# Moving down-products, row products, the ranking of experts and an overflow loop in a mixture-of-experts kernel

## The chip, the core and the metric

The kernel runs on one core of one Trainium2 chip. Its engines are TensorE (PE; its weight loads are shown apart as PEld), VectorE (DVE), ScalarE (ACT), GpSimd (POOL) and SyncE (SP), which issues most DMAs. The metric is device time in microseconds (us), the median of several executions. Rows of a trace come from one profiled execution, counted from the start of its span.

## The reference

The reference is one layer of a decoder, for 512 rows of 1024 channels. Its first part mixes tokens (a gated recurrence and a sparse attention, merged and projected), and the change does not touch it. The second part is a mixture of experts:

```python
N_GROUPS = 4
EXP_PER_GROUP = 8          # 32 experts; one group per row, two experts in it
TOPK_IN_GROUP = 2
D_EXPERT = D_MODEL // 2    # 512
...
# per routed row:  h = silu(row @ exp_w1[e]) * (row @ exp_w3[e]);  y = h @ exp_w2[e]
# a row's two results are weighted and added; then residual and LayerNorm
```

The two commented lines put the expert's formula in short. With 512 rows and two experts each there are 1024 routed rows over 32 experts, unevenly. All of it is float32.

## The kernel before, in words

**Units.** The expert part works through 13 units, called first to thirteenth here (`n` = 0 to 12 in the code). A unit is 128 slots, shared by one, two or four experts. First `rank` sorts the experts by the number of their rows, so that the busiest get a whole unit, the middle ones half of one and the others a quarter. The first two units hold experts 0 to 3 and do not depend on the ranking; all later units load the experts that the ranking names. Rows beyond an expert's slots go to the overflow loop (below).

**A unit's work.** `gather` makes the products pgx, which pick the unit's rows out of x by one-hot matrices (pm) and leave them transposed in xe; it serves two coming units at a time. `up` (L1461) makes two sets of products p, rows by exp_w1 and by exp_w3; ACT takes the silu of the first set and DVE multiplies it by the second (s, L1469). `down_lhs` (L1472) transposes s (pat) and the weighted one-hot matrix pw (ptw) on PE; ACT copies the former (aT, L1477). `down` (L1496) makes the down-products py, weighs them (y) and splits them in two parts (yh, yl). `combine` (L1508) multiplies these by the 0/1 matrix pT and adds the result to the four row blocks of acc: the *row products* pcb, 16 per unit. A unit's row products are made one unit later. In the program the order on PE is, for each unit: up-products, row products of the unit before, gather (after every second unit), transposes, down-products.

**Weights.** An expert has 12 tiles of 128x1024 float32 (512 KB): four each of exp_w1, exp_w3 and exp_w2. They stand in a ring Q of 36 buffers, of which 12 hold other things at that time. SP issues their loads (L1270; of the last unit's exp_w2 L1267, cut by quarters of the columns) in program order, and each waits until the products that read the buffer's tile before are done. SP has eight DMA counters, named DMAHW0 to DMAHW7 in the listings below, and a load waits for the one that had its counter before.

**The sort.** `sort_experts` (L1371) stands behind the first unit's up-products. Four products on PE count the rows of each expert (pcnt), then DVE works out ranks, slots (`look`, which makes the one-hot's `lk`) and the overflow list. For the units to come `rel_to` (L1329) and `one_hots` prepare the matrices on DVE.

**The end.** In `quarter_up` (L1603) and `quarter_add` (L1613) the last unit's down-products are made in four quarters of 256 columns; behind each stand 16 row products, which add both the last unit's rows and those of the twelfth unit (`todo`) to acc. `squares` (L1600) on ACT prepares the norms, and the closing work from L1625 on scales and stores the rows. Between the third and the fourth quarter's row products stands `overflow` (L1521): a loop (L1526) that runs nblk times, once per block of 128 rows beyond their experts' slots, and loads each block's weights for itself. In the runs shown nblk is zero: no instruction of the loop's body is in the trace, only its branches. Two broadcasts of norm vectors (`row_bc`) are loaded by POOL ahead of the last unit's transposes.

All instructions stand in the order in which the code writes them; no scheduler moves them.

Of the kernel before, what the change touches and what calls it, by code (L numbers as in the profile page):

```python
# [21 lines left out]
F32 = mybir.dt.float32  # L22
# [5 lines left out]
OP = mybir.AluOpType  # L28
# [3 lines left out]
NT = T // 128  # L32
# [109 lines left out]
def hybrid_kernel(ctx, tc, a, out, dbg=None, stop=None):  # L142
# [17 lines left out]
    def S(name, dt=F32):  # L160
        return big.tile([128, 512], dt, name=name, tag="S", bufs=24)
# [1206 lines left out]
    ovf = cp.tile([128, 64], F32, name="ovf")  # L1368
    ovi = cp.tile([128, 64], I32, name="ovi")

    def sort_experts():  # L1371

        pcnt = PS("pcnt")
        for j in range(NT):
            mm(pcnt[:, 0:32], onesb, mb[:, j, :], j == 0, j == NT - 1)
        srt = S("srt")
        key, rk, base, cap_, t6, cnt = (srt[:, 32 * j:32 * j + 32] for j in range(6))
        V.tensor_copy(cnt, pcnt[:, 0:32])
        V.scalar_tensor_tensor(key, cnt, 32.0, iota[:, 0:32], op0=OP.mult, op1=OP.subtract)
        V.tensor_scalar(key[:, 0:4], iota[:, 0:4], -1.0, -100.0, op0=OP.mult, op1=OP.add)  # L1380
        big2 = S("cmpm").bitcast(BF).rearrange("p (e f) -> p e f", e=32)
        V.tensor_tensor(big2, key[:, None, :].to_broadcast([128, 32, 32]),
                        key.rearrange("p (e o) -> p e o", o=1).to_broadcast([128, 32, 32]), op=OP.is_gt)
        V.tensor_reduce(rk.rearrange("p (e o) -> p e o", o=1), big2, axis=AX.X, op=OP.add)

        V.tensor_tensor(big2, rk[:, None, :].to_broadcast([128, 32, 32]),
                        iota[:, 0:32].rearrange("p (e o) -> p e o", o=1).to_broadcast([128, 32, 32]), op=OP.is_equal)
        V.tensor_tensor(big2, big2, iota[:, None, 0:32].to_broadcast([128, 32, 32]), op=OP.mult)
        V.tensor_reduce(ovf[:, 0:32].rearrange("p (j o) -> p j o", o=1), big2, axis=AX.X, op=OP.add)
        V.tensor_copy(ovi[:, 0:32], ovf[:, 0:32])  # L1390
        t1 = S("t1")[:, :256].rearrange("p (c i e) -> p c i e", c=2, i=NT)

        def look(dst, table):

            V.tensor_tensor(t1, oh2, table[:, None, None, :].to_broadcast([128, 2, NT, 32]), op=OP.mult)
            V.tensor_reduce(dst.rearrange("p c (i o) -> p c i o", o=1), t1, axis=AX.X, op=OP.add)

        V.tensor_scalar(cap_, rk, 2.0, 64.0, op0=OP.is_lt, op1=OP.mult)
        V.tensor_scalar(t6, rk, 12.0, 32.0, op0=OP.is_lt, op1=OP.mult)
        V.tensor_add(cap_, cap_, t6)
        V.tensor_scalar(t6, rk, 28.0, 32.0, op0=OP.is_ge, op1=OP.mult)
        V.scalar_tensor_tensor(cap_, cap_, 32.0, t6, op0=OP.add, op1=OP.add)
        V.tensor_scalar(base, rk, 64.0, 128.0, op0=OP.mult, op1=OP.add)
        V.scalar_tensor_tensor(base, rk, 128.0, base, op0=OP.mult, op1=OP.min)
        V.tensor_scalar(t6, rk, 32.0, 512.0, op0=OP.mult, op1=OP.add)
        V.tensor_tensor(base, base, t6, op=OP.min)
        look(bst, base)  # L1410
        look(capt, cap_)
        V.tensor_tensor(far, pos, capt, op=OP.is_ge)
        V.tensor_add(slots, bst, pos)
        V.scalar_tensor_tensor(slots, far, 1e5, slots, op0=OP.mult, op1=OP.add)
        probe("slots", slots)


        ov = S("ov")
        need, incl, st0, t5 = ov[:, 0:32], ov[:, 32:64], ov[:, 64:96], ov[:, 96:128]
        V.tensor_sub(t5, cnt, cap_)  # L1420
        V.tensor_scalar(need, t5, 0.0, None, op0=OP.is_gt)
        for j in range(1, 4):
            V.scalar_tensor_tensor(need, t5, 128.0 * j, need, op0=OP.is_gt, op1=OP.add)
        V.tensor_tensor_scan(incl, need, need, 0.0, OP.add, OP.max)
        V.tensor_sub(st0, incl, need)
        look(ob, st0)
        V.scalar_tensor_tensor(oslots, ob, 128.0, pos, op0=OP.mult, op1=OP.add)
        V.tensor_sub(oslots, oslots, capt)
        V.tensor_scalar(far, far, 1e5, -1e5, op0=OP.mult, op1=OP.add)
        V.tensor_add(oslots, oslots, far)  # L1430
        le = S("le").bitcast(BF)[:, 0:NOV * 32].rearrange("p (j e) -> p j e", j=NOV)
        V.tensor_tensor(le, incl[:, None, :].to_broadcast([128, NOV, 32]),
                        iota[:, 0:NOV].rearrange("p (j o) -> p j o", o=1).to_broadcast([128, NOV, 32]), op=OP.is_le)
        V.tensor_copy(ovf[:, 32:33], incl[:, 31:32])
        V.tensor_reduce(ovf[:, 33:33 + NOV].rearrange("p (j o) -> p j o", o=1), le, axis=AX.X, op=OP.add)
        V.tensor_copy(ovi[:, 32:33 + NOV], ovf[:, 32:33 + NOV])
# [21 lines left out]
        t = w[k // 2]  # L1458
        return t[k % 2] if isinstance(t, list) else t[:, (k % 2) * 512:(k % 2 + 1) * 512]

    def up(xe, n0, ws, rhs=k1):  # L1461
        lhs = lambda k: xe[k // 2][:, k % 2, :]
        p1 = PS("p1")
        unit_mm(p1, lhs, n0, ws["exp_w1"], rhs, 8)
        s1 = S("s1")
        A.activation(s1, p1, AF.Silu)
        p3 = PS("p3")
        unit_mm(p3, lhs, n0, ws["exp_w3"], rhs, 8)
        V.tensor_mul(s1, s1, p3)  # L1469
        return s1  # L1470
# [22 lines left out]
        V.tensor_sub(yl, y, yh.bitcast(F32))  # L1493
        return yh, yl

    def down(act, ws, pw, rhs=k1):  # L1496
        aT, pT, cs_ = down_lhs(act, pw)
        pys = [PS("py") for _ in range(2)]
        m = 128 // len(ws["exp_w2"])
        for k in range(4):  # L1500
            for half in range(2):
                for x, w in enumerate(ws["exp_w2"]):
                    mm(pys[half][m * x:m * x + m, :], aT[:, k, m * x:m * x + m], rhs(w, 2 * k + half), k == 0, k == 3,
                       pos=(0, m * x) if m < 128 else None)
        ys = [weighted_halves(pys[half], cs_, half * 512, 512) for half in range(2)]
        return pT, ys
# [14 lines left out]
    def overflow():  # L1521
        ocnt = cp.tile([128, 1], F32, name="ocnt")
        V.memset(ocnt, 0.0)
        nonlocal S
        S, s_ring = (lambda name, dt=F32: Q(name, dt)[:, 0:512]), S
        with tc.For_i(0, nblk, 1) as jb:  # L1526
            ex = nc.sync.value_load(ovi[0:1, ds(jb + 33, 1)], min_val=0, max_val=NE - 1)
            rel = rel_to(oslots, ocnt)
# [12 lines left out]
                return get  # L1541
            act = up(xe, 0, {n: [stream(n)] for n in ("exp_w1", "exp_w3")}, lambda w, k: w(k))
            combine(*down(act, {"exp_w2": [stream("exp_w2")]}, pw, lambda w, h: w(h)))

            for i in range(NT):
                V.tensor_reduce(sums[:, i, 0:3], acc[i][:, 0:768].rearrange("p (q n) -> p q n", q=3), axis=AX.X, op=OP.add)
                squares(i, 0)
        S = s_ring


    units = [-2, -1] + ORDER
    todo, hots, nblk = None, None, None
    ws = w_first
    for n, u in enumerate(units):
        pw = weighted(rels.pop(u))
        nxt = units[n + 1:n + 3] if n % 2 == 1 else []
        if nxt:
            for x in nxt:
                rels[x] = rel_to(slots, 128.0 * x)
            hots = one_hots([rels[x] for x in nxt])  # L1560
        if n == 4:

            nblk = nc.values_load_multi_w_load_instructions(
                ovi[0:1, 32:33], min_val=0, max_val=NOV - 1,
                skip_runtime_bounds_check_because="a sum of fewer blocks than NOV")[1][0]
        act = up(xe, (n % 2) * 128, ws)
        if n == 0:
            sort_experts()
        w_now = ws
        if n + 1 < len(units):  # L1570
            v_ = units[n + 1]
            if v_ < 0:
                es = (2, 3)
            elif v_ < 2:
                es = (ev(v_),)
            elif v_ < 7:
                es = (ev(2 * v_ - 2), ev(2 * v_ - 1))
            else:
                es = tuple(ev(4 * v_ - 16 + x) for x in range(4))
            ws = load_unit(es, quarters=n + 2 == len(units))  # L1580
        if todo is not None and n + 1 < len(units):
            combine(*todo)
        if nxt:
            xe = gather(hots)
        if n + 1 < len(units):
            todo = down(act, w_now, pw)
    l2g = row_bc("l2g", a["ln2_g"])
    l2b = row_bc("l2b", a["ln2_b"])

# [22 lines left out]

    def quarter_add(q, y, i):  # L1613

        o = q % 2 * 256
        terms = [(todo[0], t[:, o:o + 256]) for t in todo[1][q // 2]] + [(pT, t) for t in y]
        pc_ = PS("pcb")[:, 0:256]
        for j, (p_, t) in enumerate(terms):
            mm(pc_, p_[:, i * 128:(i + 1) * 128], t, j == 0, j == 3)
        z = acc[i][:, q * 256:(q + 1) * 256]  # L1620
        V.tensor_tensor_reduce(out=z, in0=z, in1=pc_, scale=1.0, scalar=0.0, op0=OP.add, op1=OP.add,  # L1621
                               accum_out=sums[:, i, q:q + 1])
# [35 lines left out]
            V.tensor_scalar(nsh, sums[:, :, 0], -1.0 / 256, None, op0=OP.mult)  # L1658
    squares(2, 0)
    squares(3, 0)  # L1660
    overflow()
    A.preload_act_table_set("natural_log_exp_and_others")
    V.tensor_reduce(l3[:, :, 4:5], sums[:, :, 0:3], axis=AX.X, op=OP.add)
    for i in range(NT):
# [42 lines left out]
```

## Time and profile before

| | |
|---|---|
| median of 3 runs | 1275.64 us (1275.42 to 1276.81) |
| profiled execution | 1276.27 us, span 1274.4 us |
| PE busy | 1176.6 us (92%) |
| DVE busy | 697.5 us (55%) |
| ACT busy | 425.5 us (33%) |
| POOL busy | 123.4 us (10%) |
| DMA | 297 MB, mean 233 GB/s |

The shares are means over the whole span. The expert part is the last 500 us or so, and the page's slices, each a fortieth of the span (31.9 us), show how engines and DMA stand in it. Each product of two float32 operands has two rows in the trace (x32 for 16 products in the order); durations hold for the pairs as they stand.

### The profile page before, as it was taken

The numbers are of one execution on the slowest core, as the hardware profiler recorded it, in microseconds if no ns is written. First come the engines' busy times: TensorE is split into PE (matmuls) and PEld (weight loads), VectorE is DVE, ScalarE is ACT, GpSimd is POOL, SyncE is SP. The second block draws the span as 40 slices with busy tenths as digits, with TensorE's granted clock in tenths as the row PEclk, the third lists the DMA queues.
The fourth block names the chain that finished last, engine by engine and source line by source line (L and its number), as shares of the span: only waits on it lengthen the run. The fifth ranks groups of instructions, "written<-read, shape, count | busy, mean of one in ns | idle before, by whom it ended". The sixth has DMA issues, their size and how long they took to land. (4 is left out here: it accounts for less than half of the span.)

```text
span 1274.4 us, 18563 instructions
## 1 busy us (share of the span) xinstructions
PE 1176.6 (92%) x6663; PEld 813.2 (64%) x6663; DVE 697.5 (55%) x1621; ACT 425.5 (33%) x897; POOL 123.4 (10%) x179
## 2 busy tenths in 40 slices
PE   5999999999999999999979969999999899899993
PEld 4788898778888888878758953525335235143442
DVE  5564988887565665314596786534143143313436
ACT  5233666664536254554131421201102012010113
POOL 3011111111110011010250140000000000000002
PEclk9999999999999999999999979999999999999997
DMA  9954413324334153345425279799999999999991
GB/s 324 295 152 139 120 52 117 104 87 129 112 109 142 45 174 100 92 147 156 132 66 182 79 301 361 297 411 408 409 409 409 409 409 408 409 409 407 403 346 68
DMA packets 140863, 297.15 MB, mean 233 GB/s; under 512 B 11099, under 2 KB 82979, under 8 KB 140768
## 3 DMA queue, kind: packets, MB, share of 16 engines
q1 hardware_dynamic: 131296, 268.57, 57.5%
q0 software_dynamic: 8704, 25.00, 6.2%
q10 hardware_dynamic: 768, 2.37, 0.5%
q8 instruction: 53, 0.87, 0.3%
q14 instruction: 42, 0.34, 0.1%
HBM read 293.76 MB, written 4.76 MB: 234 GB/s over the span
## 5 line engine op out<-in xcount | busy, mean ns | idle before, releaser
L184 PE MATMUL p<-ew,xe 128*32 128x512 f32 (+1 forms) x960 | 209.0, 599 | 14.9 <-DMA ew<-in_exp_w_dram 14.4
L277 DVE TENSOR_TENSOR wl<-wst,wh 128x1024 fp32r<-128x1024 f32 (+1 forms) x93 | 124.2, 1365 | 75.1 <-ACT wh L276 74.4
L184 PEld LDWEIGHTS p<-ew,xe 128*32 128x32 f32 (+1 forms) x960 | 55.1, 122 | 166.7 <-DMA ew<-in_exp_w_dram 85.4
L184 PE MATMUL py<-ew,aT 128*32 128x512 f32 (+2 forms) x496 | 96.6, 570 | 7.8 <-DMA ew<-in_exp_w_dram 5.2
L276 ACT ACTIVATE wh<-wst 128x1024 fp32r<-128x1024 f32 (+1 forms) x94 | 93.0, 1030 | 29.5 <-POOL wst L275 16.6
L1469 DVE TENSOR_TENSOR s<-s,p 128x512 f32<-128x512 f32 x13 | 8.9, 687 | 142.3 <-PE p L184 136.4
L184 PEld LDWEIGHTS py<-ew,aT 128*32 128x32 f32 (+1 forms) x496 | 27.1, 122 | 70.5 <-issue 34.2
L1490 DVE SCALAR_TENSOR_TENSOR y<-py,cs,g2b 128x512 f32<-128x512 f32 (+1 forms) x28 | 19.9, 710 | 85.5 <-PE py L184 75.4
L1492 ACT ACTIVATE yh<-y 128x512 fp32r<-128x512 f32 (+1 forms) x28 | 16.8, 599 | 139.4 <-DVE y L1490 132.8
L1355 ACT ACTIVATE xe<-pgx,sm 128x256 f32<-128x256 f32 (+1 forms) x48 | 26.3, 547 | 106.2 <-PE pgx L182 106.2
L182 PE MATMUL pgx<-pm,xhh 128*128 128x256 f32 (+1 forms) x224 | 58.3, 299 | 1.5 <-DVE pm L1242 1.5
L182 PE MATMUL pgx<-pm,xhl 128*128 128x256 f32 (+1 forms) x224 | 57.6, 296 | 0.0
L1516 DVE TENSOR_TENSOR acc<-acc,pcb 128x512 f32<-128x512 f32 x88 | 53.5, 679 | 0.0
L515 POOL DMA_DIRECT2D adaw<-in_ada_w_dram x64 | 34.5, 541 | 196.0 <-PE ptp L188 42.0
L182 PE MATMUL pmg<-hh,wh 128*128 128x512 f32 x128 | 50.4, 394 | 0.0
L182 PE MATMUL psg<-hh,wh 128*128 128x512 f32 x128 | 50.3, 393 | 0.0
L182 PE MATMUL psg<-hl,wh 128*128 128x512 f32 x128 | 49.9, 390 | 0.0
L182 PE MATMUL pmg<-hh,wl 128*128 128x512 f32 x128 | 49.9, 390 | 0.0
L182 PE MATMUL psg<-hh,wl 128*128 128x512 f32 x128 | 49.9, 390 | 0.0
L182 PE MATMUL pmg<-hl,wh 128*128 128x512 f32 x128 | 49.8, 389 | 0.0
L182 PE MATMUL pcb<-yh,pT 128*128 128x512 f32 (+1 forms) x120 | 44.5, 381 | 5.1 <-DVE s L1469 2.9
L182 PEld LDWEIGHTS pgx<-pm,xhh 128*128 128x128 f32 x224 | 46.1, 206 | 2.6 <-DVE pm L1242 1.9
(513 smaller groups left out, 2843.0 us busy)
## 6 DMA issues: line engine op xcount, KB each, us to landing
ew<-in_exp_w_dram SPq DMA_DIRECT2D x380, 512.0 KB, 10.1
wst<-in_w_in_dram SPq DMA_DIRECT2D x66, 512.0 KB, 4.8
adaw<-in_ada_w_dram POOLq DMA_DIRECT2D x64, 256.0 KB, 3.1
adaw<-in_ada_w_dram SPq DMA_DIRECT2D x16, 512.0 KB, 9.2
wst<-in_w_br_hg_dram SPq DMA_DIRECT2D x8, 512.0 KB, 3.8
wst<-in_w_br_nsa_dram SPq DMA_DIRECT2D x8, 512.0 KB, 4.5
wst<-in_w_out_dram SPq DMA_DIRECT2D x8, 512.0 KB, 4.9
ext_d<-ext_d POOLq DMA_DIRECT2D x1, 2560.0 KB, 17.3
```

The source lines that it names most:

```text
L182: PE.matmul(o, l, r, start=start, stop=stop)
L184: PE.matmul(o, l, r, start=start, stop=stop, tile_position=pos)
L276: A.activation(wh, self.w[j], AF.Copy)
L277: (sub or V).tensor_sub(wl, self.w[j], wh.bitcast(F32))
L515: P_.dma_start(w, ada[:, k, 2048 + j * 512:2560 + j * 512])
L1355: A.activation(xe[k // 2][:, k % 2, 0:128 * u], pgx, AF.Identity, bias=sm2[:, 0, k:k + 1], scale=sm2[:, 1, k:k + 1])
L1469: V.tensor_mul(s1, s1, p3)
L1490: V.scalar_tensor_tensor(y, py, cs_, g2b[c0 // 512][:, c0 % 512:c0 % 512 + n], op0=OP.mult, op1=OP.mult)
L1492: A.activation(yh, y, AF.Copy)
L1516: V.tensor_add(acc[i][:, s_], acc[i][:, s_], pc_)
```

## The change

Five things change places in the code. The ranking (`rank_experts`) stands ahead of the first unit's up-products; the rest of the sort (`place_experts`) stands in the first unit's `down`, behind its transposes. The one-hots of coming units are made inside `down` as well, and the gather stands behind the down-products. The first unit's row products are made together with the second unit's, in the third unit; from there on, a unit's row products stand between the next unit's up-products and its transposes, as before. The twelfth unit's row products stand between the two halves of the thirteenth's up-products, and no longer in the quarters. The overflow loop stands behind the gather for the thirteenth unit, ahead of its up-products; of that unit's loads, exp_w1 and exp_w3 are issued ahead of the loop and exp_w2 behind it. In the loop's body two tiles are kept in ring S's place by halves of Q, which has no part in a run without overflow.

```diff
--- before.py
+++ after.py
@@ -1368,7 +1368,7 @@
     ovf = cp.tile([128, 64], F32, name="ovf")
     ovi = cp.tile([128, 64], I32, name="ovi")
 
-    def sort_experts():
+    def rank_experts():
 
         pcnt = PS("pcnt")
         for j in range(NT):
@@ -1388,6 +1388,10 @@
         V.tensor_tensor(big2, big2, iota[:, None, 0:32].to_broadcast([128, 32, 32]), op=OP.mult)
         V.tensor_reduce(ovf[:, 0:32].rearrange("p (j o) -> p j o", o=1), big2, axis=AX.X, op=OP.add)
         V.tensor_copy(ovi[:, 0:32], ovf[:, 0:32])
+        return srt
+
+    def place_experts(srt):
+        key, rk, base, cap_, t6, cnt, need, incl, st0, t5 = (srt[:, 32 * j:32 * j + 32] for j in range(10))
         t1 = S("t1")[:, :256].rearrange("p (c i e) -> p c i e", c=2, i=NT)
 
         def look(dst, table):
@@ -1415,8 +1419,6 @@
         probe("slots", slots)
 
 
-        ov = S("ov")
-        need, incl, st0, t5 = ov[:, 0:32], ov[:, 32:64], ov[:, 64:96], ov[:, 96:128]
         V.tensor_sub(t5, cnt, cap_)
         V.tensor_scalar(need, t5, 0.0, None, op0=OP.is_gt)
         for j in range(1, 4):
@@ -1458,12 +1460,14 @@
         t = w[k // 2]
         return t[k % 2] if isinstance(t, list) else t[:, (k % 2) * 512:(k % 2 + 1) * 512]
 
-    def up(xe, n0, ws, rhs=k1):
+    def up(xe, n0, ws, rhs=k1, mid=None):
         lhs = lambda k: xe[k // 2][:, k % 2, :]
         p1 = PS("p1")
         unit_mm(p1, lhs, n0, ws["exp_w1"], rhs, 8)
         s1 = S("s1")
         A.activation(s1, p1, AF.Silu)
+        if mid:
+            mid()
         p3 = PS("p3")
         unit_mm(p3, lhs, n0, ws["exp_w3"], rhs, 8)
         V.tensor_mul(s1, s1, p3)
@@ -1493,8 +1497,10 @@
         V.tensor_sub(yl, y, yh.bitcast(F32))
         return yh, yl
 
-    def down(act, ws, pw, rhs=k1):
+    def down(act, ws, pw, rhs=k1, mid=None):
         aT, pT, cs_ = down_lhs(act, pw)
+        if mid:
+            mid()
         pys = [PS("py") for _ in range(2)]
         m = 128 // len(ws["exp_w2"])
         for k in range(4):
@@ -1522,7 +1528,18 @@
         ocnt = cp.tile([128, 1], F32, name="ocnt")
         V.memset(ocnt, 0.0)
         nonlocal S
-        S, s_ring = (lambda name, dt=F32: Q(name, dt)[:, 0:512]), S
+        s_ring, half = S, {}
+
+        def s_loop(name, dt=F32):
+
+            if name not in ("ow", "xe", "pm"):
+                return s_ring(name, dt)
+            if name in half:
+                return half.pop(name)
+            q = Q(name, dt)
+            half[name] = q[:, 512:1024]
+            return q[:, 0:512]
+        S = s_loop
         with tc.For_i(0, nblk, 1) as jb:
             ex = nc.sync.value_load(ovi[0:1, ds(jb + 33, 1)], min_val=0, max_val=NE - 1)
             rel = rel_to(oslots, ocnt)
@@ -1541,49 +1558,61 @@
                 return get
             act = up(xe, 0, {n: [stream(n)] for n in ("exp_w1", "exp_w3")}, lambda w, k: w(k))
             combine(*down(act, {"exp_w2": [stream("exp_w2")]}, pw, lambda w, h: w(h)))
-
-            for i in range(NT):
-                V.tensor_reduce(sums[:, i, 0:3], acc[i][:, 0:768].rearrange("p (q n) -> p q n", q=3), axis=AX.X, op=OP.add)
-                squares(i, 0)
         S = s_ring
 
+    hots = None
 
     units = [-2, -1] + ORDER
-    todo, hots, nblk = None, None, None
+    todo, nblk, srt = [], None, None
     ws = w_first
     for n, u in enumerate(units):
         pw = weighted(rels.pop(u))
-        nxt = units[n + 1:n + 3] if n % 2 == 1 else []
-        if nxt:
-            for x in nxt:
-                rels[x] = rel_to(slots, 128.0 * x)
-            hots = one_hots([rels[x] for x in nxt])
+        if n == 0:
+            srt = rank_experts()
         if n == 4:
 
             nblk = nc.values_load_multi_w_load_instructions(
                 ovi[0:1, 32:33], min_val=0, max_val=NOV - 1,
                 skip_runtime_bounds_check_because="a sum of fewer blocks than NOV")[1][0]
-        act = up(xe, (n % 2) * 128, ws)
-        if n == 0:
-            sort_experts()
-        w_now = ws
-        if n + 1 < len(units):
-            v_ = units[n + 1]
-            if v_ < 0:
-                es = (2, 3)
-            elif v_ < 2:
-                es = (ev(v_),)
-            elif v_ < 7:
-                es = (ev(2 * v_ - 2), ev(2 * v_ - 1))
-            else:
-                es = tuple(ev(4 * v_ - 16 + x) for x in range(4))
-            ws = load_unit(es, quarters=n + 2 == len(units))
-        if todo is not None and n + 1 < len(units):
-            combine(*todo)
+
+        def add_up():
+            while todo:
+                combine(*todo.pop(0))
+        last = n + 1 == len(units)
+        act = up(xe, (n % 2) * 128, ws, mid=add_up if last else None)
+        if last:
+            break
+        v_ = units[n + 1]
+        if v_ < 0:
+            es = (2, 3)
+        elif v_ < 2:
+            es = (ev(v_),)
+        elif v_ < 7:
+            es = (ev(2 * v_ - 2), ev(2 * v_ - 1))
+        else:
+            es = tuple(ev(4 * v_ - 16 + x) for x in range(4))
+        w_now, quarters = ws, n + 2 == len(units)
+        ws = load_unit(es, hi=8 if quarters else 12)
+        if n > 1:
+            add_up()
+        nxt = units[n + 1:n + 3] if n % 2 == 1 else []
+
+        def to_come():
+
+            nonlocal hots
+            if n == 0:
+                place_experts(srt)
+            if nxt:
+                for x in nxt:
+                    rels[x] = rel_to(slots, 128.0 * x)
+                hots = one_hots([rels[x] for x in nxt])
+        todo.append(down(act, w_now, pw, mid=to_come))
         if nxt:
             xe = gather(hots)
-        if n + 1 < len(units):
-            todo = down(act, w_now, pw)
+        if quarters:
+            overflow()
+            ws = load_unit(es, 8, 12, ws, quarters=True)
+    w_now = ws
     l2g = row_bc("l2g", a["ln2_g"])
     l2b = row_bc("l2b", a["ln2_b"])
 
@@ -1612,11 +1641,9 @@
 
     def quarter_add(q, y, i):
 
-        o = q % 2 * 256
-        terms = [(todo[0], t[:, o:o + 256]) for t in todo[1][q // 2]] + [(pT, t) for t in y]
         pc_ = PS("pcb")[:, 0:256]
-        for j, (p_, t) in enumerate(terms):
-            mm(pc_, p_[:, i * 128:(i + 1) * 128], t, j == 0, j == 3)
+        for j, t in enumerate(y):
+            mm(pc_, pT[:, i * 128:(i + 1) * 128], t, j == 0, j == 1)
         z = acc[i][:, q * 256:(q + 1) * 256]
         V.tensor_tensor_reduce(out=z, in0=z, in1=pc_, scale=1.0, scalar=0.0, op0=OP.add, op1=OP.add,
                                accum_out=sums[:, i, q:q + 1])
@@ -1658,7 +1685,6 @@
             V.tensor_scalar(nsh, sums[:, :, 0], -1.0 / 256, None, op0=OP.mult)
     squares(2, 0)
     squares(3, 0)
-    overflow()
     A.preload_act_table_set("natural_log_exp_and_others")
     V.tensor_reduce(l3[:, :, 4:5], sums[:, :, 0:3], axis=AX.X, op=OP.add)
     for i in range(NT):
```

How this moves instructions shows in the program's order on each engine. The first place is PE at the second unit: p are up-products, pcb row products, pgx the gather, pat and ptw transposes, py down-products, and the number behind p is the tile's. Before:

```order
L184 MATMUL p_7620<-ew,xe 64x512 x16
L184 MATMUL p_7639<-ew,xe 64x512 x16
L182 MATMUL pcb<-yh,pT 128x512
L182 MATMUL pcb<-yl,pT 128x512
...
L182 MATMUL pgx<-pm,xhh 128x256
L182 MATMUL pgx<-pm,xhl 128x256
...
L188 MATMUL pat<-cst,s_7637 128x128 x4
L188 MATMUL ptw<-cst,pw 128x128 x4
L184 MATMUL py<-ew,aT 64x512 x16
```

and now:

```order
L184 MATMUL p_7589<-ew,xe 64x512 x16
L184 MATMUL p_7608<-ew,xe 64x512 x16
L188 MATMUL pat<-cst,s_7606 128x128 x4
L188 MATMUL ptw<-cst,pw 128x128 x4
L184 MATMUL py<-ew,aT 64x512 x16
L182 MATMUL pgx<-pm,xhh 128x256
L182 MATMUL pgx<-pm,xhl 128x256
```

The 16 row products have gone from this place, and the gather has gone behind the down-products.

The second order listing is SP at the overflow loop, with the counters that an instruction waits for. ew are weight tiles, of 128x1024 for exp_w1 and exp_w3 of the last unit and of 128x4x256 for its quarters of exp_w2. Before:

```order
L1267 DMA ew<-in_exp_w_dram 128x4x256 [waits DMAHW3_49,PE_49]
L1267 ISA
L1267 DMA ew<-in_exp_w_dram 128x4x256 [waits DMAHW4_49,PE_49]
L1526 COMPARE_AND_BRANCH
L1526 UNCONDITIONAL_BRANCH [waits SP_sequencer_49,DMAHW0_49,DMAHW1_49,DMAHW2_49,DMAHW3_49,DMAHW4_49,DMAHW5_49,DMAHW6_49,DMAHW7_49]
```

and now:

```order
L1270 DMA ew<-in_exp_w_dram 128x1024 [waits DMAHW3_49,PE_49]
L1270 ISA
L1270 DMA ew<-in_exp_w_dram 128x1024 [waits DMAHW4_49,PE_49]
L1543 COMPARE_AND_BRANCH
L1543 UNCONDITIONAL_BRANCH [waits SP_sequencer_49,DMAHW0_49,DMAHW1_49,DMAHW2_49,DMAHW3_49,DMAHW4_49,DMAHW5_49,DMAHW6_49,DMAHW7_49]
...
L1267 ISA
L1267 DMA ew<-in_exp_w_dram 128x4x256
```

The loop, line 1543 in the changed kernel, now has the last unit's exp_w1 and exp_w3 ahead of it and its exp_w2 behind it. The branch that leaves it waits for all eight counters, as it did.

The third place is PE from the loop on, now:

```order
L182 MATMUL pgx<-pm,xhl 128x128
L1543 COMPARE_AND_BRANCH
L1543 UNCONDITIONAL_BRANCH x2
...
L184 MATMUL p_10968<-ew,xe 64x512 x16
L182 MATMUL pcb<-yh,pT 128x512
L182 MATMUL pcb<-yl,pT 128x512
...
L184 MATMUL p_11019<-ew,xe 64x512 x16
```

What is left out at the first "..." is the body. The row products of the twelfth unit stand between the two sets of up-products of the thirteenth.

## Rows read from the trace of the kernel before

**Rows 1.** The page's slices: busy tenths of the DMA engines in 40 slices.

```profile
DMA  9954413324334153345425279799999999999991
```

**Rows 2.** Windows: stretch, length, busy us of PE, PEld, DVE, ACT, POOL, granted clock, DMA share, GB/s.

```profile
810.00:815.00 5.00, 5.00 (x38) 5.00 (x38) 2.24 (x4) 2.56 (x5) 0.00 (x0) 0.84 0.92 368
815.00:820.00 5.00, 4.75 (x36) 3.71 (x36) 0.69 (x1) 3.05 (x7) 0.00 (x0) 1.00 0.02 8
820.00:825.00 5.00, 5.00 (x26) 1.72 (x24) 0.00 (x0) 0.00 (x0) 0.00 (x0) 1.00 0.68 224
825.00:830.00 5.00, 5.00 (x44) 1.33 (x44) 3.53 (x8) 1.26 (x2) 0.00 (x0) 1.00 0.97 326
830.00:1220.00 390.00, 367.17 (x1774) 155.06 (x1768) 134.96 (x306) 50.72 (x98) 0.00 (x0) 1.00 1.03 408
```

**Rows 3.** Waits of SP's queue, 765 to 830 us: total, times, longest.

```profile
SPq L1270 <- PE py L184: 20.7, 7, 13.4
```

**Rows 4.** PE's timeline at the second unit: start, duration; idle time before, its releaser.

```profile
787.29 13.90 PE L184 MATMUL p<-ew,xe 128*64 128x512 f32 x64
...
807.52 0.50 PE L182 MATMUL pcb<-yh,pT 128*128 128x512 f32 x1 [2.93 <-DVE s L1469]
...
817.38 0.65 PE L188 MATMUL pat<-cst,s 128*128 128x128 f32 x4
...
818.72 7.09 PE L184 MATMUL py<-ew,aT 128*64 128x512 f32 x32 [0.25 <-ACT aT L1477]
```

**Rows 5.** DVE's timeline at the second unit.

```profile
778.14 0.69 DVE L1469 TENSOR_TENSOR s<-s,p 128x512 f32<-128x512 f32 x1 [8.68 <-PE p L184]
...
801.90 0.24 DVE L1329 TENSOR_SCALAR rel<-lk 128x8 f32<-128x8 f32 x2
```

**Rows 6.** PE's timeline from the twelfth unit's up-products to the loop.

```profile
1198.68 1.93 PE L184 MATMUL p<-ew,xe 128*64 128x512 f32 x6 [0.20 <-DMA ew<-in_exp_w_dram]
...
1204.32 0.22 PE L182 MATMUL pgx<-pm,xhh 128*128 128x128 f32 x1
...
1212.87 7.09 PE L184 MATMUL py<-ew,aT 128*64 128x512 f32 x32 [0.31 <-ACT aT L1477]
...
1219.79 14.78 PE L184 MATMUL p<-ew,xe 128*64 128x512 f32 x64
...
1236.86 3.67 PE L184 MATMUL py<-ew,aT 128*64 128x256 f32 x32 [0.25 <-ACT aT L1477]
...
1242.56 1.95 PE L184 MATMUL py<-ew,aT 128*64 128x256 f32 x16
...
1246.54 1.95 PE L184 MATMUL py<-ew,aT 128*64 128x256 f32 x16
...
1252.75 0.39 PE L182 MATMUL pcb<-yh,pT 128*128 128x256 f32 x1 [2.15 <-issue]
```

**Rows 7.** Weight loads on SP: those from 830 to 1220; time to landing from 680 to 900.

```profile
L1270 SPq DMA_DIRECT2D ew<-in_exp_w_dram x301: 332/333/651, 830.1 to 1219.1; - x151
...
DMA to landing us min/median/max: 3.5/10.1/11.6
```

**Rows 8.** Windows before the second unit and in its row products, columns as in rows 2.

```profile
755.00:760.00 5.00, 4.19 (x20) 3.79 (x20) 4.35 (x24) 0.00 (x0) 0.92 (x1) 0.50 0.43 172
760.00:765.00 5.00, 4.57 (x22) 3.88 (x24) 2.21 (x5) 2.04 (x4) 0.00 (x0) 0.61 0.01 2
...
808.00:812.00 4.00, 4.00 (x22) 3.89 (x21) 4.00 (x8) 0.73 (x2) 0.00 (x0) 0.57 1.03 410
```

**Rows 9.** DVE's and ACT's timelines around the loop.

```profile
1253.37 0.17 DVE L1663 TENSOR_REDUCE l<-sums 128x4 f32<-128x12 f32 x1 [2.07 <-issue]
...
1256.30 0.16 DVE L1625 SCALAR_TENSOR_TENSOR l<-sqs,l 128x2 f32<-128x2 f32 x1
...
1249.38 0.71 ACT L1600 ACTIVATE sq<-acc,nsh 128x512 f32<-128x512 f32 x1
...
1252.37 1.28 ACT L1662 ACT_TABLE_LOAD   x1 [1.34 <-DVEq L1526]
```

## The prediction

> **What bounds the kernel now.** I read the page's slices first: from the 24th on the DMA engines are at 0.9 of their time in almost every slice [rows 1]. There the expert weights come in, and the cut by stretches gives their rate: 408 GB/s from 830 to 1220 us, with a DMA share of 1.03 [rows 2]. PE looks busy too, but the up-products of the last unit but one end in a piece of six that waited for a landing, like the four pieces before it, at 1198.68 [rows 6]: PE follows the stream. So the end of the expert stage is the stream's start, plus its volume, plus its gaps, plus what stands behind the last landing.
>
> There are two gaps. In the first (2 GB/s in 760 to 765 [rows 8]) the loads wait for buffers that only the first unit's up-products free. In the second the stream delivers 368, 8, 224 and 326 GB/s in the four stretches from 810 to 830 [rows 2]; against 408 that is 0.5 + 4.9 + 2.3 + 1.0 = 8.7 us lost. The waits of SP's queue name the cause: 13.4 us in one piece for a down-product (py) [rows 3]. The next buffers are the second unit's down-weights, and its down-products start at 818.72, though its up-products ended at 801.2: in between stand 16 row products of the first unit, which wait 2.93 us for DVE, and the gather for the next two units [rows 4].
>
> At the end PE is the late one: up-products from 1219.79, transposes, quarter products from 1236.86, then the loop that does nothing (2.15 us of idle PE behind it), then the norms [rows 6, 9]. The profiled execution took 1276.27 us at a span of 1274.4; the median of the runs is 1275.64, 0.6 below it, and I take that off at the end.
>
> **Second unit: the gap goes, worth 8.7 us of stream.** Its down-products now stand behind its up-products. Up-products end at 801.2 as before; s, transposes and copies take 2.3 us (as from 1234.6 to 1236.86 [rows 6]), so py runs from 803.5 to 810.6 and frees the eight tiles before the stream would run dry at 814.5 (368 of 408 GB/s in the five from 810). They last 8 x 1.28 = 10.2 us, to 824.7 (1.28 us is one 512 KB tile at 408 GB/s). The next buffers need the up-products of unit three, which need the gather, which needs the one-hots. These are 18 short DVE operations. They start at 801.90 [rows 5] and stand ahead of s, 0.7 us, which ends when the row products go on at 807.5 [rows 4]: 4.9 us. Now they stand behind the second unit's pT: 805 to 810. So the gather runs from 810.6 to about 819 (817.38 less 808 in the rows, part of it at half clock) and unit three frees its first tiles some 2 us later, at 821; with 3.5 us to land (the least in rows 7) that is just in time. The second part of the sort stays on DVE behind the first unit's up-products, where it stood. The first part now stands ahead of s, in the 8.68 us that DVE was idle there [rows 5]: nothing, and what it no longer takes behind s comes to the second part. Its four products on PE stand ahead of the first up-products: 0.26 us, 0.4 at the half clock that rules there [rows 8]. Net: the stream is 8.7 - 0.4 = 8.3 us earlier.
>
> The remaining units add no gap: gather and down-products change places, the sum on PE is the same, and PE waits for landings. Unit three gets 32 row products instead of 16, some 5 us of DVE more, but its own 16 down tiles need 20 us to land: hidden.
>
> **The loop: from nothing to a stop of PE.** The second order listing shows it. SP leaves the loop's skip only when all eight counters of its DMA queue are full, that is, when each load issued so far has landed; every engine waits for SP there. Before, nothing was in flight at that point. Now the 16 up-weight tiles of the last unit are: the last is issued at 1219.1 and lands 10.1 us later, at 1229.2 [rows 7], less 8.3 = 1220.9. PE comes there earlier: up-products of unit 12 end at 1200.6 - 8.3 = 1192.3, then row products 3.7 (1200.6 to 1204.32), gather and transposes 8.6 (to 1212.87), down-products 6.9 (to 1219.79) [rows 6] = 1211.5. It stands for 9.4 us. The empty loop took DVE 2.07 us, from 1251.30 on, and PE's next product came at 1252.75, 1.4 us behind that [rows 6, 9]; I take 1.4, since PE is what counts. PE starts at 1222.3 instead of 1219.8: **+2.5**.
>
> **The last unit's up-products.** They took 14.8 us with small waits for landings; without, 13.9 as in the second unit [rows 4]: **-0.9**. The row products of unit 12, which before were added inside the quarters, now stand between the two halves: 16 products, 3.7 us as above: **+3.7**.
>
> **The clock.** From 755 to 760 PE worked at the half clock, and for 3.9 of the next 5 us (a mean of 0.61), and around 808, after a wait of 2.93, for 3.4 of 4 us (0.57) [rows 4, 8]. A stop of 9 us is long by that measure. If 3.4 to 8 us of the restart run at half speed, the loss is 1.7 to 4.0 us; if the clock holds, 0. The products behind the stop wait for nothing, as at 808, so I take a value nearer the short one: **+2.6**. The Trainium skill ("TensorE: Matmul & The Clock Gate", section on HAM oscillation) says that a wait for a DMA between stretches of products makes the next stretch start cold; the two rows agree. By it the term stays in the sum; without it the sum below is 2.6 smaller.
>
> **The quarters.** Their weights are issued after the loop, at about 1222. Eight loads at 1.28 us or a little more and a start of 3.5 us land by 1237 (the two broadcasts of POOL may add 3); py needs the first at 1244.8 (1222.3 + 13.9 + 3.7 + 2.6 + 2.3): hidden, with 5 us in hand. PE's cycle per quarter was 1246.54 - 1242.56 = 3.98 us, of which 2.0 for 16 row products; eight remain: 1.0 less, three cycles: 3.0. The loop's 2.15 goes too: 5.1. But ACT becomes last. The four quarters and three sets of row products on PE are 3.67 + 2 x (1.1 + 2.0) = 9.8 us; ACT is done with the last yh 0.9 later (as 1249.38 is to the end of the py from 1246.54), and then has two squares of 0.9, the table load of 1.28 and two squares [rows 6, 9]. So the scalar that opens the closing work comes 15.6 us after the first py, where it came at 1256.30 - 1236.86 = 19.4: **-3.8**.
>
> **Sum:** 2.5 - 0.9 + 3.7 + 2.6 - 3.8 = +4.1 us. 1276.27 + 4.1 = 1280.4; less 0.6: **1279.8**. The 8.3 us of stream are spent on a PE that must stand until the last tile is in, and then has more to do.
>
> **Rivals.**
> Loads in flight do not hold the loop. For it: SP's loads run by themselves, and the loop was never seen with any in flight. Then PE passes at 1211.5 + 1.4 = 1212.9, needs 13.9 + 3.7, and ends the up-products at 1230.5 instead of 1234.6, with its clock up: -4.1 - 3.8 = -7.9, or 1267.7. Against it: the waits are in the listing. 0.11.
> The stop is cheaper: the clock holds, or the chain behind the loop is shorter. Then +4.1 - 2.6 = +1.5 or less, 1277.1 and below, no change that can be told. For it: no row has PE stopped by a loop for 9 us. Against it: the two dips. 0.19.
> The gap at 815 stays, because DVE delivers the one-hots late (the row products before waited 2.93 us for it [rows 4]) and the gather ends after 824.7, where the eight tiles are used up. Then the stream is not earlier, and the whole stop moves: +4.1 + 8.3 = +12.4, 1288. It needs 6 us of delay on DVE that I do not see. 0.06.
> My own case, between: 0.64, with its bounds at +1.5 (clock holds) and +6.2 (clock 4.0, exit 2.1).
>
> **The numbers.** A change under 0.2% (2.6 us) cannot be told from none: 1273.1 to 1278.2. Slower is my case and the third rival, 0.70; same is the second, 0.19; faster the first, 0.11. The range leaves out the first and the third: from 1275.0 (the stop cheap, and 2 us more saved behind it) to 1285.0.
>
> **What would show it.** Right: DMA at 408 GB/s through 810 to 830 and the second unit's py from about 803; then PE idle for some 9 us ahead of the loop's branch, at about 1211 to 1222, DMA idle for some 4 us behind it, a granted clock of 0.5 when products resume, row products between the two halves of the last up-products, and 15 to 16 us from the first quarter product to the closing work. Wrong: products resuming before the last up-weight tile has landed (the first rival), a gap at 815 (the third), or quarters that wait for their weights.

## The result and the profile after

The changed kernel takes 1282.25 us (median of 5, 1281.96 to 1285.61) beside 1275.76 for the kernel before: a ratio of 1.0053, 95% interval 1.0039 to 1.0068. In a later run it stood at 1282.30 beside 1277.57: 1.0046, interval 1.0029 to 1.0063. It is slower, as forecast, and by 6.5 us instead of 4.2; the time lies inside the range. The profiled execution took 1282.88 us, at a span of 1281.1.

The gap in the weight stream is gone. These are the stretches of [rows 2] (length, busy us of PE, PEld, DVE, ACT and POOL, granted clock, DMA share, GB/s) after the change:

```profile
810.00:815.00 5.00, 5.00 (x33) 3.05 (x30) 3.78 (x10) 0.73 (x2) 0.00 (x0) 1.00 1.03 410
815.00:820.00 5.00, 5.00 (x44) 5.00 (x43) 3.44 (x10) 3.82 (x8) 0.00 (x0) 1.00 1.03 410
820.00:825.00 5.00, 5.00 (x50) 1.85 (x52) 0.00 (x0) 0.81 (x2) 0.00 (x0) 1.00 1.02 407
```

407 to 410 GB/s right through, where 8 and 224 stood before. SP's queue (total wait, times, longest) now waits at most 4.0 us for a down-product, not 13.4 [rows 3]:

```profile
SPq L1270 <- PE py L184: 4.9, 2, 4.0
```

The cause is in PE's timeline (start, duration, idle time before with its releaser). The second unit's down-products stand 13 us earlier than in [rows 4]; the gather follows at 812.67, without a wait:

```profile
805.66 7.09 PE L184 MATMUL py<-ew,aT 128*64 128x512 f32 x32 [0.25 <-ACT aT L1481]
```

The last up-weight tile is therefore issued at 1213.6 instead of 1219.1 [rows 7], and takes 10.0 us to land (one row per operation: count, durations in ns, first and last start; then the times to landing):

```profile
L1270 SPq DMA_DIRECT2D ew<-in_exp_w_dram x4: 332/333/333, 1209.8 to 1213.6; - x4
...
DMA to landing us min/median/max: 10.0/10.0/10.1
```

Then the lead is lost. PE has done its gather by 1214.39 and stands until 1224.51, 0.9 us after the last of these tiles has landed at 1223.6; its first 32 product rows take 10.00 us, the second 32 take 7.09:

```profile
1224.51 10.00 PE L184 MATMUL p<-ew,xe 128*64 128x512 f32 x32 [10.11 <-SPq L1543]
...
1238.30 7.09 PE L184 MATMUL p<-ew,xe 128*64 128x512 f32 x32
...
1247.68 3.67 PE L184 MATMUL py<-ew,aT 128*64 128x256 f32 x32 [0.25 <-ACT aT L1481]
```

The windows show the stop on every engine, DMA running dry at its end, and the granted clock at 0.50, the lower of its two levels (1.2 GHz), when products come back:

```profile
1210.00:1215.00 5.00, 4.39 (x40) 4.25 (x39) 0.57 (x2) 3.15 (x8) 0.00 (x0) 1.00 1.02 405
1215.00:1220.00 5.00, 0.00 (x0) 0.00 (x0) 0.00 (x0) 0.00 (x0) 0.00 (x0) 0.68 0.72 284
1220.00:1225.00 5.00, 0.49 (x2) 0.29 (x4) 0.66 (x3) 0.00 (x0) 0.26 (x1) 0.50 0.05 19
1225.00:1230.00 5.00, 5.00 (x14) 1.42 (x12) 2.17 (x7) 0.00 (x0) 0.87 (x2) 0.50 0.62 237
1230.00:1235.00 5.00, 5.00 (x22) 1.61 (x19) 0.00 (x0) 0.44 (x1) 0.00 (x0) 0.96 0.98 302
```

The tail is shorter, as expected: the DVE operation that opens the closing work, and that waits for ACT's squares, comes 15.3 us after the first quarter product, where it came 19.4 after it [rows 6, 9]:

```profile
1262.95 0.16 DVE L1652 SCALAR_TENSOR_TENSOR l<-sqs,l 128x2 f32<-128x2 f32 x1 [0.22 <-ACT sq L1629]
```

### The profile page after: what moved, and what is told of

It is laid out like the page before. It is cut to its first block, busy times and chain, and to the rows that moved or that the text cites. A ratio compares the mean times of both kernels' runs of the same rounds, so it can differ in the third digit from the quotient of the medians.

```text
span 1281.1 us, 18558 instructions
## 1 busy us (share of the span) xinstructions
PE 1177.3 (92%) x6647; PEld 813.4 (63%) x6647; DVE 702.9 (55%) x1629; ACT 423.2 (33%) x897; POOL 122.5 (10%) x179
## 5 line engine op out<-in xcount | busy, mean ns | idle before, releaser
L184 PE MATMUL p<-ew,xe 128*32 128x512 f32 (+1 forms) x960 | 205.6, 604 | 23.3 <-DMA ew<-in_exp_w_dram 12.7
L1481 ACT ACTIVATE aT<-pat 128x512 f32<-128x512 f32 x13 | 7.8, 597 | 186.0 <-PE pat L188 186.0
L1522 DVE TENSOR_TENSOR acc<-acc,pcb 128x512 f32<-128x512 f32 x96 | 58.3, 681 | 8.0 <-PE pcb L182 8.0
L182 PEld LDWEIGHTS pgx<-pm,xhl 128*128 128x128 f32 x224 | 45.2, 202 | 0.5 <-issue 0.5
## 6 DMA issues: line engine op xcount, KB each, us to landing
ew<-in_exp_w_dram SPq DMA_DIRECT2D x380, 512.0 KB, 10.1
```

Of the source, the lines that this page charges most:

```text
L182: PE.matmul(o, l, r, start=start, stop=stop)
L184: PE.matmul(o, l, r, start=start, stop=stop, tile_position=pos)
L1481: A.activation(aT, at_.rearrange("p (f s) -> p f s", f=4), AF.Copy)
L1522: V.tensor_add(acc[i][:, s_], acc[i][:, s_], pc_)
```

## Experiments

The theory: moving the second unit's down-products gives the stream some 8 us, and the loop takes them back, since it holds all engines until every load in flight has landed. One other explanation: the loop costs its two microseconds wherever it stands, and the rest is the new place of the row products. Another: the gap at 815 was hidden anyway. Ratios are to the kernel before on the same chip, and where the experiments ran it took 1277.57 to 1278.58 us, 1.8 to 2.8 more than the 1275.76 beside the changed kernel. The expectations were worked out from 1275.8 and 1282.3, so whether a time in us met them can be told only to within that much. The profiles are therefore compared by their *rest* as well: the span less the start of the first unit's up-products, which differs from execution to execution. Each rest comes from one execution; the two of the changed kernel differ by 1.3. The row of that start, for the kernel before and for the changed one:

```profile
764.04 13.95 PE L184 MATMUL p<-ew,xe 128*64 128x512 f32 x64
```

```profile
766.25 13.95 PE L184 MATMUL p<-ew,xe 128*64 128x512 f32 x64
```

| profile of | start | span | rest |
|---|---|---|---|
| before | 764.0 | 1274.4 | 510.4 |
| changed | 766.3 | 1281.1 | 514.9 |
| changed, second run | 766.3 | 1279.9 | 513.6 |
| loop back at the end | 763.3 | 1267.0 | 503.8 |
| only the loop ahead | 765.1 | 1285.3 | 520.2 |
| no loop | 765.2 | 1267.1 | 501.9 |
| only the second unit's order | 765.2 | 1269.4 | 504.3 |
| 8 tiles ahead of the loop | 763.7 | 1269.3 | 505.6 |
| 12 tiles | 763.7 | 1273.4 | 509.7 |
| 20 tiles | 763.9 | 1286.2 | 522.3 |
| loop ahead, rows in the quarters | 763.9 | 1277.3 | 513.4 |
| loop at the end, rows in the quarters | 768.2 | 1272.1 | 503.9 |

**Loop back at the end.** The changed kernel with one part undone (the loop's body, which never runs, is also as in the kernel before):

```diff
-        ws = load_unit(es, hi=8 if quarters else 12)
+        ws = load_unit(es, quarters=quarters)
...
-        if quarters:
-            overflow()
-            ws = load_unit(es, 8, 12, ws, quarters=True)
...
     squares(3, 0)
+    overflow()
```

> The changed kernel, with only the overflow loop put back to where it stood in the kernel before (between the third and the fourth quarter's row products), and the last unit's loads issued in one go. Theory (the loop holds all engines until every load in flight has landed): in the changed kernel PE stands from 1214.4 to 1224.5 and works at the half clock behind it (32 product rows in 10.0 us where they need 7.0). Both go, 10.1 + 3.0; the loop at the end costs some 2 again as in the kernel before. 1282.3 - 13.1 + 2 = 1271, from 1269.5 to 1273. Rival (the stop has little to do with the loads, and the cost is the row products between the up-products): the loop costs its 2 us at either place, so 1280 to 1283.

Measured: 1270.53 us, ratio 0.9945 (0.9924 to 0.9966). The rest is 503.8 us, 11.1 below the changed kernel's. The up-products follow the gather without a stop, at full clock, and the loop's own 2.2 us stand at the end:

```profile
1211.50 7.09 PE L184 MATMUL p<-ew,xe 128*64 128x512 f32 x32
...
1244.88 0.45 PE L182 MATMUL pcb<-yh,pT 128*128 128x256 f32 x1 [2.17 <-DVEq L1532]
```

The first of the other explanations falls: with the row products where the change put them, the time is 0.55% below the kernel before.

**Only the loop ahead.** The kernel before, with the loop (its unused body as in the changed kernel, and behind it the last unit's exp_w2) ahead of the last unit:

```diff
-            ws = load_unit(es, quarters=n + 2 == len(units))
+            ws = load_unit(es, hi=8 if n + 2 == len(units) else 12)
...
             todo = down(act, w_now, pw)
+        if n + 2 == len(units):
+            overflow()
+            ws = load_unit(es, 8, 12, ws, quarters=True)
...
-    overflow()
     A.preload_act_table_set("natural_log_exp_and_others")
```

> The kernel before, with only the overflow loop moved ahead of the last unit, the last unit's exp_w2 loads behind it; second unit, sort and row products as before. Theory: the stream is not earlier, the last up-weight tile lands at 1229.2, PE goes on 0.9 later at 1230.1 instead of 1219.8: +10.3. Up-products without waits -0.9, half clock behind the stop +3.0, loop gone from the end -2.1. Sum +10.3: 1286, from 1284 to 1288. Rival (loads in flight do not hold the loop): about 2 us less than before, 1273 to 1276.

Measured: 1286.15 us, ratio 1.0059 (1.0039 to 1.0079); the rest is 9.8 us longer than before, against 10.3 expected. PE stands as long as in the changed kernel, since stream and PE are both later:

```profile
1231.09 16.59 PE L184 MATMUL p<-ew,xe 128*64 128x512 f32 x64 [10.17 <-SPq L1537]
```

**No loop.** The changed kernel without the call:

```diff
         if quarters:
-            overflow()
             ws = load_unit(es, 8, 12, ws, quarters=True)
```

> The changed kernel without any overflow loop: the part of the computation that handles rows beyond their experts' slots is left out (there are none in this input). Theory: the stop of 10.1 us and the half clock's 3.0 go: 1282.3 - 13.1 = 1269, from 1267.5 to 1270.5, so about 2 below the kernel with the loop at the end. Rival (the loop's own branches cost it, about 2 us): 1280.

Measured: 1268.26 us, ratio 0.9924 (0.9902 to 0.9947); the rest is 501.9 us, 13.0 below the changed kernel's (13.1 expected) and 1.9 below that with the loop at the end. So the loop costs 13 us at its new place and 2 at its old one, for a body that never runs.

**Only the second unit's order.** The kernel before with the row products of the first unit held back, one-hots inside `down` (`to_come` makes them there) and the gather behind it:

```diff
-        if todo is not None and n + 1 < len(units):
-            combine(*todo)
-        if nxt:
-            xe = gather(hots)
-        if n + 1 < len(units):
-            todo = down(act, w_now, pw)
+        if n + 1 < len(units):
+            if n > 1:
+                while todo:
+                    combine(*todo.pop(0))
+            todo.append(down(act, w_now, pw, mid=to_come))
+        if nxt:
+            xe = gather(hots)
```

> The kernel before, with only the order of the second unit changed: down-products directly behind the up-products, the first unit's row products one unit later, one-hots behind the transposes, gather behind the down-products. Sort in one piece behind the first unit's up-products, loop at the end, the twelfth unit's row products in the quarters. Theory (PE follows the stream to the end): the gap at 815 goes, the stream is 7.7 us earlier, as between the two traces (last up-weight load 5.5 earlier with a start 2.2 later), and so is the end: 1275.8 - 7.7 = 1268, from 1266 to 1270. Rival (the gap is hidden behind PE's own work later, or the sort in one piece makes the one-hots late, so that the gap moves to the next unit): 1273 to 1276.

Measured: 1270.44 us, ratio 0.9939 (0.9917 to 0.9962), where 7.7 us of 1275.8 make 0.9940. The second of the other explanations falls, and the sort in one piece does no harm that shows. The end of the last up-products is 7.6 us earlier, counted from the first; the rest only 6.1, since the row products behind the loop at the end ran at a granted clock of 0.57, which the kernel before, with nearly the same stop (2.14 us here, 2.15 there), had at 1.00 (same columns as above; first this kernel, then the kernel before):

```profile
1246.00:1250.00 4.00, 3.69 (x16) 3.49 (x16) 1.45 (x7) 2.82 (x5) 0.00 (x0) 0.57 0.01 2
```

```profile
1252.00:1256.00 4.00, 2.18 (x16) 1.98 (x16) 2.37 (x12) 2.91 (x5) 0.00 (x0) 1.00 0.01 2
```

**More and fewer loads ahead of the loop.** The changed kernel, with 8, 12 or 20 of the last unit's 24 tiles issued ahead of the loop instead of 16 (h is 4, 6 or 10, for each of two experts):

```diff
-        ws = load_unit(es, hi=8 if quarters else 12)
+        ws = load_unit(es, hi=h if quarters else 12, quarters=quarters)
...
-            ws = load_unit(es, 8, 12, ws, quarters=True)
+            ws = load_unit(es, h, 12, ws, quarters=True)
```

With 8:

> The changed kernel, with only the last unit's exp_w1 (8 tiles) issued ahead of the loop, exp_w3 and exp_w2 behind it. Theory (the stop lasts until the last load issued ahead has landed): by the changed kernel's trace the eighth tile lands at 1223.6 - 8 x 1.28 = 1213.4, before PE comes at 1214.4. The stop shrinks to about 1, the clock holds. exp_w3 is issued 3 later, at 1218.6, and its last tile lands at 1231.9; the up-products end at 1233.5 instead of 1245.4: 1282.3 - 11.9 = 1270.4, from 1269 to 1273. Rival (the loop itself stops the engines, whatever is in flight): no change, 1280 to 1284.

With 12:

> The changed kernel, with exp_w1 and the first half of exp_w3 (12 tiles) of the last unit issued ahead of the loop. Theory: the last of them lands at 1223.6 - 4 x 1.28 = 1218.5, PE goes on at 1219.4, a stop of 5.0 instead of 10.1. If a stop of 5 us leaves the clock up, the up-products end at 1237.5 and the time is 1274.4; if the half clock follows as behind the 10 us (3.0 lost), 1277.4. Rival (the length does not hang on the loads): 1282.

With 20:

> The changed kernel, with exp_w1, exp_w3 and half of exp_w2 (20 tiles) of the last unit issued ahead of the loop. Theory: the last of them lands 4 x 1.28 = 5.1 later, at 1228.7, PE goes on at 1229.6: a stop of 15.2, and 1282.3 + 5.1 = 1287.4, from 1286 to 1289. Rival (PE waits for the last up-weight tile and not for all loads in flight): no change, 1282.

Measured: 1271.66, 1276.64 and 1287.75 us; ratios 0.9955 (0.9939 to 0.9970), 0.9987 (0.9977 to 0.9996) and 1.0073 (1.0059 to 1.0087). The first up-products behind the loop, with the stop in brackets, for 8, 12 and 20 tiles:

```profile
1213.96 8.75 PE L184 MATMUL p<-ew,xe 128*64 128x512 f32 x32 [2.20 <-issue]
```

```profile
1217.34 9.45 PE L184 MATMUL p<-ew,xe 128*64 128x512 f32 x32 [5.30 <-SPq L1543]
```

```profile
1229.65 9.92 PE L184 MATMUL p<-ew,xe 128*64 128x512 f32 x32 [17.17 <-SPq L1543]
```

8, 12, 16 and 20 tiles make stops of 2.2, 5.3, 10.1 and 17.2 us. With 20 PE has every up-weight it needs by 1223.0: the last of them was issued at 1211.6, and no load of that stretch took more than 11.4 us to land:

```profile
L1270 SPq DMA_DIRECT2D ew<-in_exp_w_dram x25: 332/333/336, 1180.3 to 1211.6; - x25
...
DMA to landing us min/median/max: 9.6/10.1/11.4
```

PE stands to 1229.65 all the same, 1.1 us after the last exp_w2 tile issued ahead of the loop has landed at 1228.5 (issued at 1217.1, 11.4 to land): what holds it is the last load in flight, not the one it will use. From 12 to 16 the stop grows by 4.8, near the 5.1 that four tiles take at the stream's rate; from 16 to 20 by 7.1 (the quarters' tiles took 11.1 to 11.4 us to land, not 10, which is some 1.3 of the 2.0 beyond 5.1). With 8 only the loop's own 2.2 are left. By the rest, 8 tiles save 9.3 us (11.9 expected), 12 save 5.2 (7.9 expected if the clock stayed up, 4.9 if not), and 20 cost 7.4 (5.1 expected, a miss). The clock's price, against 7.09 us at full speed, is 1.7, 2.4, 2.9 and 2.8 us: it comes with the short stop too, where it was expected to be nothing.

**The twelfth unit's row products back in the quarters**, in the kernel with the loop at the end and in the changed one (`quarter_add` as before, and):

```diff
-        act = up(xe, (n % 2) * 128, ws, mid=add_up if last else None)
+        act = up(xe, (n % 2) * 128, ws)
...
-        for j, t in enumerate(y):
-            mm(pc_, pT[:, i * 128:(i + 1) * 128], t, j == 0, j == 1)
+        for j, (p_, t) in enumerate(terms):
+            mm(pc_, p_[:, i * 128:(i + 1) * 128], t, j == 0, j == 3)
```

> The kernel of the run with the loop at the end, with the twelfth unit's row products back in the quarters, as in the kernel before. Theory: 3.9 us of row products leave the up-products; the three cycles of the quarters get 1.0 longer each, which takes back 3.0 less what ACT had in hand (1.3): the closing work comes 2.2 earlier at most and 0.9 at least, so 1268.3 to 1269.6 against 1270.5. Rival (in the quarters they fill waits and cost nothing): 1266.6.

> The changed kernel, loop ahead of the last unit as there, with the twelfth unit's row products back in the quarters. Theory: the stop (10.1) and the half clock behind it stay; the up-products end 3.9 earlier, the quarters take 3.0 more less some 1.3 that ACT had in hand: 0.9 to 2.2 less than the changed kernel beside it, 0.07 to 0.17%. The exp_w2 tiles, issued some 3 behind the restart, are then needed 3.9 earlier and have 0.6 in hand (4.5 before). Rival (they come late): no gain or up to 1 slower.

> The changed kernel once more, beside the one with the rows in the quarters on the same chip: the same ratio to the kernel before as at first, 1.004 to 1.007; a stop of 10.1 and 2.9 lost to the half clock. If the later start of the first up-products (766.25 against 764.04) came from the change, it is there again; if it is a matter of the execution, it differs, as in the other runs (763.3 to 768.2).

Measured: loop at the end, 1272.51 us, ratio 0.9951 (0.9934 to 0.9968), no difference from 0.9945; the expectation missed. Its rest equals the other's (503.9 to 503.8). Counted from the first up-products, the first quarter's product comes 3.7 us earlier; the three longer cycles take back 2.8 of it, near the 3.0 expected. The other 0.8, and 0.8 more, go into the row products behind the loop: 16 instead of 8 stand there, and DVE's additions wait for them. In both kernels they run at the lower clock level (granted clock 0.57 in 1249 to 1253 here, 0.56 in 1244.8 to 1246.8 there). Loop ahead, 1279.07 us beside 1282.30 for the changed kernel on the same chip: ratios 1.0010 (0.9998 to 1.0022) and 1.0046. The 3.2 us are more than 0.9 to 2.2. The rest gives only 0.2 (513.4 to 513.6) against the second execution of the changed kernel, whose clock price was 1.2 lower, and 1.5 against the first, whose clock price was the same 2.9. 2.4 us of the difference between this profile and that of the second execution lie ahead of the first up-products. My worry over exp_w2 was wrong: the first quarter's tiles land at 1232.3 and are wanted at 1242.0.

The changed kernel, run again as it is, had its stop again, 10.12 us, but a clock price of 1.7 instead of 2.9:

```profile
1224.56 8.75 PE L184 MATMUL p<-ew,xe 128*64 128x512 f32 x32 [10.12 <-SPq L1543]
```

Four kernels that keep the loop beat both the kernel before and the changed one (loop at the end with the rows in either place, second unit alone, 8 tiles ahead: 0.9945, 0.9951, 0.9939, 0.9955); no difference between them can be told. The second unit's order alone gives as much as any of the others.

## Why the prediction was right

The mechanism came in: the stream gains its lead, and the loop takes it back by holding PE until the last tile is in. The first rival (loads in flight do not hold the loop) is shown wrong by the run with 20 tiles, the third (the gap stays) by the windows. Of the second (the stop is cheaper) the clock's price of 1.7 in the second execution is the nearest sign, at the edge of the bounds of 1.7 to 4.0.

The steps, counted from the start of the first up-products. The prediction's 0.4 for the four counting products ahead of them is taken out of its lead and its restart and stands in a row of its own:

| step | predicted | measured |
|---|---|---|
| start of the first up-products | +0.4 | +2.2 (766.25 - 764.04) |
| stream earlier | 8.7 | 7.7 (last up-weight tile 5.5 earlier, the start 2.2 later) |
| PE stands until the last tile has landed | 9.4 | 9.2 (1214.39 to 1223.6) |
| from that landing to PE | 1.4 | 0.9 |
| restart of PE | +2.1 | +2.5 (1224.51 - 1219.79 - 2.2) |
| up-products without waits | -0.9 | -0.7 (20.88 - 14.78 - 3.9 - 2.9) |
| row products in the middle | +3.7 | +3.9 |
| half clock behind the stop | +2.6 | +2.9, in a second execution +1.7 |
| quarters and tail | -3.8 | -4.2 (15.27 - 19.44) |
| sum from the restart on | +3.7 | +4.5 (514.9 - 510.4) |

The size was 2.5 us short: 1282.25 against 1279.8. The steps miss about 0.8 of it, and even that hides a lead 1.0 smaller and an exit 0.5 shorter than forecast, which offset each other at the restart. Some 1.8 more stand ahead of the first up-products, where the sum had 0.4 for the counting products (they took 0.26, from 765.99 to 766.25) and nothing else. Of the 2.2 us, 1.5 are there before anything that the change moves (the last product of the token mixing's output starts at 736.7, before at 735.2). The test set for this was whether the late start comes again in the second execution, and it did (766.31). But seven other kernels have the changed order up to that point, and theirs start between 763.3 and 768.2: the order does not enforce it. Why both profiles of the changed kernel itself start at 766.3 stays open.

That the time still fell inside the range is in part luck. The measured +6.5 lies just above the +6.2 that the prediction worked out as the most for its own case (1281.8 us); it adds up no step for the rest of the range, up to 1285.0. Two smaller slips changed nothing: the rows give 8.9 us at the half clock ahead of 765, not 8, and the sum for the quarters holds two sets of row products where its sentence says three.

The clock's step rested on two rows in which products came back at the lower level after a wait. Neither wait was for a DMA: ahead of the first PE had waited 3.12 us for ACT and 4.63 for DVE (its rows at 744.88 and 751.62), ahead of the second 2.93 for DVE. The Trainium skill ("TensorE: Matmul & The Clock Gate", section on HAM oscillation) states the same for waits on a DMA, and all six stops of 5 us and more read here agree, at a price of 1.7 to 2.9 us.

## What to carry to other kernels

In this kernel the loop was a barrier for every load in flight on SP's queue, also with a count of zero: 2.2 us with all loads landed, 10.1 and 17.2 with 16 and 20 tiles issued ahead of it. Look for such waits in the program's order, and put a loop that has them where the queue is empty anyway, or issue ahead of it only what has landed when the engines arrive. A lead won in a stream is worth what the next barrier leaves of it; look for the first place where all engines must wait for the same queue. And price a stop by the clock behind it too: here 1.7 to 2.9 us ahead of the up-products, behind 2.2 us of stop as behind 17.

## What was not expected of the hardware

The clock's price shows no clear link to the length of the stop: 1.7 us after 2.2, 2.4 after 5.3, 2.9 and 1.7 after 10.1 in two executions of one kernel, 2.8 after 17.2. With one execution for most lengths and 1.2 us between two of the same kernel, a weak link can't be excluded. Stops of 2.14 to 2.17 us at the end left the clock at 1.00 in the kernel before, and in three others it stood at 0.56 to 0.57 behind them.

SP issued its first load behind the loop 3.2 us after PE had gone on (PE's row at 1224.51 is above), where the prediction had it at the restart:

```profile
1227.73 8.20 SPq L1267 DMA_DIRECT2D ew<-in_exp_w_dram  x8
```

In the repeated run it was 3.0 (1227.60 to 1224.56). The Trainium skill ("Runtime: NRT & Kernel Launch", section on instruction fetch mechanics) says that a taken branch to code that is not at hand must fetch it first; that would fit. Two packets of a queue of the kind "instruction" (q14) move between 1225 and 1226, and at least one within about 2 us of the restart in each other run with the loop ahead. Which engine they are for is not in the trace, so the cause stays open. It cost nothing, since the exp_w2 tiles had time in hand.
